# Modulation columns by one VectorE operation out of PSUM, two column blocks moved ahead of a matmul pass, one weight load moved ahead of another load

## The chip, the cores and the metric

The kernel runs on one core of a Trainium2 chip. The metric is the device time of one execution in microseconds (us). A core has a matmul engine (TensorE, in the profile PE, with its weight loads as PEld), a vector engine (VectorE, DVE), an activation engine (ScalarE, ACT), a general engine (GpSimd, POOL) and a queue engine that issues most transfers (SyncE, SP). Each engine works through its own instructions in order. SBUF is the on-chip memory, PSUM the memory that TensorE writes into.

## The reference

One transformer block on x of 1024 tokens by 1024 features, float32. What concerns this change is its beginning:

```python
mod = silu(c) @ w_ada + b_ada                      # 6 x 1024 numbers
sh_a, sc_a, g_a, sh_f, sc_f, g_f = split(mod, 6)
h = rms_norm(x, g_mix) * (1.0 + sc_a) + sh_a       # scale and shift by feature
proj = h @ w_in                                    # 1024 x 2240
# two kinds of attention on proj, w_out, residual times g_a,
# then rms_norm * (1 + sc_f) + sh_f, SwiGLU, residual times g_f, final rms_norm
```

So the first product needs, for every feature, two numbers that come from a product of c with w_ada: a scale g_mix * (1 + b + sc) and a shift b + sh. The features are cut into 8 blocks of 128, and the numbers of one block are two columns, one number for each of the 128 partitions.

## The kernel before

**The first pass.** A float32 product is made of three passes: each operand is split into a high part and the rest, and high*high, low*high and high*low are added in PSUM. In the code z = 0, 1, 2 are these three: pass (k, z) multiplies feature block k. `g1(0, ...)` (line 484 and on) does it for the first 512 tokens. For each k it runs the passes z = 0, 1, 2 over five output tiles at once (5 matmuls of 128x512 each, L481), and after each pass calls `between`, here `g1_0`, which puts the preparation of later blocks at that place of the program. Pass (k, 0) needs `hh` (high part of h, block k) and `whi` (high part of the weights), pass (k, 1) `hl`, pass (k, 2) `wlo`.

**What is made for one block k.** `h_T(0, k)` transposes x on TensorE into PSUM (L423). `ada_sum(c, ...)` (L255, L257) sums silu(c)[i] * w_ada[i] on VectorE, eight tiles one after the other, for a chunk c of columns: chunks 0 and 1 are one block wide, chunks 2, 4 and 6 are two blocks wide, so chunk 4 serves blocks 4 and 5. The partial sums lie in PSUM, the last one goes to SBUF as `acc`. `ada_cols(c)` adds the 128 partitions with small matmuls against ones (L270) and so makes the columns in PSUM. `acol_of` (L262 to L264) makes scale and shift from them and stores them in `acol`. `h_split(0, k)` applies both on ScalarE (L430, in place in PSUM), makes `hh` there (L162, a cast) and `hl` on VectorE (L158). The weights are split by `whi` (a cast on ScalarE, L303, that of tile 0 on GpSimd, L301) and `wlo` (a subtraction on GpSimd, L158).

**Order.** `pn` keeps what it is given in the order in which the code is written, so on each engine the work of this phase stands as `g1_0` calls it. `keep_busy` (L202) runs matmuls on constants into an unused tile. Transfers of this phase are issued by SP in the order of `load_x`, `load_ada` and `load_w` (from line 310). Tiles of 512 KB share one pool of 49 slots.

**After it** follow the rest of the projections, attention, the output product and the feed-forward part; the change touches none of them.

Of the kernel before, what the change touches and what calls it, by code (L numbers as in the profile page):

```python
# [11 lines left out]
ALU = mybir.AluOpType  # L12
# [85 lines left out]
def emit(ctx, tc, a, out, dbg=None, rec=None):  # L98
    nc = rec or tc.nc
# [11 lines left out]
    def slot(shape, dt, name):  # L111
        n = nm(name)
        if rec:
            rec.alloc(n)
        return sp.tile([P] + list(shape), dt, name=n, tag="s", bufs=NBUF)
# [37 lines left out]
    def pn(ins):  # L153
        if pinned[0]:
            pin(ins)
# [23 lines left out]
    V = con.tile([P, 78], F32, name="V")  # L179
    V1 = con.tile([P, 48], F32, name="V1")  # L180
    cact = con.tile([P, 8], F32, name="cact")
    acol = con.tile([P, 2, 8], F32, name="acol")
# [48 lines left out]
    def load_ada(k, q):  # L231
        n = CHUNKS[k]
        per = 4 // n
        src = a["ada_a"][k] if n == 1 else a["ada_b"][k // 2 - 1]
        adar[k, q] = slot([per, 256 * n], F32, "ada")
        pn(ld(out=adar[k, q], in_=src[:, q * per:(q + 1) * per, :]))
# [6 lines left out]
    def ada_sum(k, kts, sb=False):  # L243
        w = 256 * CHUNKS[k]
        if 0 in kts:
            adac[k] = [None, slot([512], F32, "acc"), None]
        e = adac[k]
        if not sb and e[0] is None:
            e[0] = psb()
        for kt in kts:  # L250
            src = ada_kt(k, kt)
            c = cact[:, kt:kt + 1]
            o = e[1] if sb or kt == 7 else e[0]
            if kt == 0:
                pn(nc.vector.tensor_scalar(out=o[:, 0:w], in0=src, scalar1=c, scalar2=None, op0=ALU.mult))  # L255
            else:
                pn(nc.vector.scalar_tensor_tensor(out=o[:, 0:w], in0=src, scalar=c, in1=e[2][:, 0:w], op0=ALU.mult, op1=ALU.add))  # L257
            e[2] = o

    def acol_of(k, n, sc, sh):  # L260
        ac = acol[:, 0, k:k + n]
        pn(nc.vector.tensor_tensor(out=ac, in0=sc, in1=V1[:, 8 + k:8 + k + n], op=ALU.add))  # L262
        pn(nc.vector.tensor_tensor(out=acol[:, 1, k:k + n], in0=sh, in1=V[:, 8 + k:8 + k + n], op=ALU.add))
        pn(nc.vector.tensor_tensor(out=ac, in0=ac, in1=V[:, 56 + k:56 + k + n], op=ALU.mult))  # L264

    def ada_cols(k):
        n = CHUNKS[k]
        ps, acc, _ = adac.pop(k)
        for s in range(2 * n):
            pn(mm(ps[:, s:s + 1], lhsT=acc[:, s * 128:(s + 1) * 128], rhs=ones[:, 0:1], start=True, stop=True))  # L270
        sc = ps[:, 0:2 * n].rearrange("p (k s) -> p s k", s=2)
        return lambda: acol_of(k, n, sc[:, 0, :], sc[:, 1, :])
# [21 lines left out]
    def load_w(k):  # L294
        raww[k] = slot([1024], F32, "raw")
        pn(ld(out=raww[k], in_=win[k * P:(k + 1) * P, 0:1024]))

    def whi(k, eng=None):
        W["s0", k] = (slot([1024], F32R, "whi"), slot([1024], F32R, "wlo"))
        if eng:  # L300
            pn(eng.tensor_copy(W["s0", k][0], raww[k]))  # L301
        else:
            pn(nc.scalar.copy(W["s0", k][0], raww[k]))  # L303

    def wlo(k):
        hi, lo = W["s0", k]
        sub(nc.gpsimd, lo, raww.pop(k), f(hi))
# [2 lines left out]
        load_x(t)  # L310
    load_ada(0, 0)
    load_ada(0, 1)
    load_ada(1, 0)
    load_w(0)
    load_ada(1, 1)
    load_w(1)
    for c in (2, 4, 6):
# [79 lines left out]
    for q in range(3):  # L397
        n = 3 if q < 2 else 2
# [21 lines left out]
    def h_T(hf, k, ts=range(4)):  # L420
        ps = hps[hf, k] = hps.get((hf, k)) or psb()
        for t in ts:
            pn(nc.tensor.transpose(ps[:, t * 128:(t + 1) * 128], xr[hf * 4 + t][:, k * 128:(k + 1) * 128], ident))  # L423

    def h_split(hf, k):
        ps = hps.pop((hf, k))
        if k % 2 == 0:
            hT[hf, k // 2] = (slot([2, 512], F32R, "hh"), slot([2, 512], F32R, "hl"))
        hi, lo = (z[:, k % 2, :] for z in hT[hf, k // 2])
        pn(nc.scalar.activation(ps, ps, AF.Identity, scale=acol[:, 0, k:k + 1], bias=acol[:, 1, k:k + 1]))  # L430
        split(ps, hi, lo)
# [107 lines left out]
    ada0((5, 6), True)  # L539
    keep_busy(4)  # L540
    acol_of(0, 1, ps0[:, 0, 0:1], ps0[:, 1, 0:1])
    ada_sum(1, range(2))
    whi(0, nc.gpsimd)
# [6 lines left out]
    def g1_0(k, z):  # L550
        if z == 0 and k < 7:
            h_T(0, k + 1)
        if z == 1 and k == 0:
            ada_sum(2, range(2))
            ada_cols(1)()
            ada_sum(2, range(2, 4))
            h_split(0, 1)
            ada_sum(2, range(4, 8))
            for j in (2, 3):
                whi(j)  # L560
                wlo(j)
        if z == 1 and k in (1, 3, 5):
            n = k + 3
            if n < 8:
                ada_sum(n, range(1))
            ada_cols(k + 1)()
            if n < 8:
                ada_sum(n, range(1, 3))
            h_split(0, k + 1)
            if n < 8:  # L570
                ada_sum(n, range(3, 6))
        if z == 1 and k in (2, 4, 6):
            h_split(0, k + 1)
            n = k + 2
            if n < 8:
                ada_sum(n, range(6, 8))
                for j in (n, n + 1):
                    whi(j)
                    wlo(j)
        if k == 6 and z == 1:  # L580
            st.ahead = 5
            st.allow(("ad", 2, 3))
            st.need(("x", 7))
# [5 lines left out]
    def g1_1(k, z):  # L589
# [4 lines left out]
        if z == 2:  # L594
            st.pump(2)

    g1(0, g1_0, g1_0t, 5)
    pinned[0] = False
    st.ahead = 4
# [87 lines left out]
    op = {}  # L687
# [80 lines left out]
    for u in range(2):  # L768
        nc.vector.tensor_tensor_reduce(out=lj, in0=lam[:, u * 128:u * 128 + 64], in1=lam[:, u * 128 + 64:u * 128 + 128],
                                       op0=ALU.mult, op1=ALU.add, scale=1.0, scalar=0.0, accum_out=lsum[:, u:u + 1])  # L770
# [782 lines left out]
```

## Time and profile before

| what | value |
|---|---|
| median of 3 executions | 1260.49 us (1259.66 to 1263.78) |
| profiled execution, its own time | 1262.53 us |
| its span, first to last instruction | 1260.5 us |
| mean granted TensorE clock | 0.982 |
| TensorE busy | 1209.6 us (96%) |
| VectorE, ScalarE, GpSimd busy | 830.9, 494.8, 439.0 us |
| first pass, blocks 0 to 7 | 16.23 to 62.5 us of the span |

The times of single instructions come from the profiled execution, whose own time is 2.0 us above its span and 2.0 us above the median. [...] In a timeline row the first number is the start, the second the time, and a bracket says how long the engine sat idle before it and what released it; rows of small float32 matmuls count each twice.

### The profile page before, as it was taken

To read this page: it belongs to the slowest core of one execution; us is meant where nothing else is said; L and a number is where in the kernel's file an instruction comes from. 1 tells how busy PE (TensorE), PEld (TensorE's weight loads), DVE (VectorE), ACT (ScalarE), POOL (GpSimd) and SP (SyncE) were. 2 spreads that over 40 slices of the span, in tenths; PEclk is the share of its full clock that TensorE was granted. 3 is DMA by queue.
4 is the path that set the end of the run, shared out by engine and by line. 5 is a ranking of instruction groups with operands and counts; after the bars stand their busy time and mean duration, and the time that the engine had idled before them with its cause. 6 is when DMAs were issued, how large, how long until landed. Compare 5 with 4: busy or idle time off the path is not lost.

```text
span 1260.5 us, 16480 instructions
## 1 busy us (share of the span) xinstructions
PE 1209.6 (96%) x5951; PEld 1016.3 (81%) x5951; DVE 830.9 (66%) x1284; ACT 494.8 (39%) x850; POOL 439.0 (35%) x492
## 2 busy tenths in 40 slices
PE   8999999999989999999899999999999999999995
PEld 6788898988779888887688888878888888878774
DVE  6552614567787778768865565655555665699997
ACT  4433314555546665214632233213233244243353
POOL 4312001655243247113465445564444620000112
PEclk9899999999999999999899999999999999999998
DMA  9672962347995434331132333322122369779543
GB/s 369 268 253 105 355 185 68 105 122 230 334 291 159 152 101 133 103 116 67 50 101 101 101 117 118 114 87 73 61 101 84 117 226 391 251 256 326 188 130 134
DMA packets 82972, 209.33 MB, mean 166 GB/s; under 512 B 7805, under 2 KB 18379, under 8 KB 82763
## 3 DMA queue, kind: packets, MB, share of 16 engines
q1 hardware_dynamic: 63611, 168.36, 40.0%
q0 software_dynamic: 6336, 23.07, 4.8%
q10 hardware_dynamic: 12944, 16.84, 3.9%
q8 instruction: 47, 0.77, 0.3%
q14 instruction: 34, 0.28, 0.1%
HBM read 164.21 MB, written 44.04 MB: 165 GB/s over the span
## 4 chain that ended last, share of the span: by engine, by line
PE 77%; DVE 12%; ACT 4%; issue 3%; DMA 2%; POOL 1%; SPq 0%; ACTq 0%; POOLq 0%; DVEq 0%
PE psb L1338 32%; PE psb L439 5%; PE psb L440 5%; PE psb L441 5%; PE psb L481 3%; PE psd L481 3%; PE psd L1485 2%; PE psd L1486 2%; PE psd L1484 2%; PE psb L1030 2%; PE psb L1485 2%; PE psb L1484 2%; PE psb L1486 2%; ACT s L949 2%; DVE dlo L158 1%
## 5 line engine op out<-in xcount | busy, mean ns | idle before, releaser
L1338 PE MATMUL psb<-ah,whi 128*128 128x512 f32 x528 | 143.6, 393 | 2.9 <-ACT uv L1367 2.6
L1338 PE MATMUL psb<-ah,wlo 128*128 128x512 f32 x528 | 141.9, 391 | 0.8 <-DVE wlo L158 0.8
L1338 PE MATMUL psb<-al,whi 128*128 128x512 f32 x528 | 141.7, 390 | 0.4 <-DVE al L158 0.4
L1361 POOL TENSOR_TENSOR cf<-cf,cf 128x512 f32<-128x512 f32 x44 | 66.4, 1510 | 190.4 <-DVE cf L1354 182.6
L1338 PEld LDWEIGHTS psb<-ah,whi 128*128 128x128 f32 x528 | 99.1, 189 | 25.0 <-ACT uv L1367 3.0
L1354 DVE TENSOR_TENSOR cf<-psb,uv 128x512 f32<-128x512 f32 x88 | 60.4, 687 | 89.0 <-PE psb L1338 87.6
L1338 PEld LDWEIGHTS psb<-ah,wlo 128*128 128x128 f32 x528 | 99.6, 189 | 22.1 <-DVE wlo L158 1.2
L1338 PEld LDWEIGHTS psb<-al,whi 128*128 128x128 f32 x528 | 99.0, 188 | 21.3 <-DVE al L158 0.8
L162 ACT CAST whi<-ssum 128x1024 fp32r<-128x1024 f32 x44 | 45.1, 1046 | 166.9 <-POOL ssum L158 166.9
L158 DVE TENSOR_TENSOR wlo<-ssum,whi 128x1024 fp32r<-128x1024 f32 x44 | 62.2, 1415 | 55.6 <-ACT whi L162 55.5
L949 ACT ACTIVATE s<-s,nb 128x640 f32<-128x640 f32 (+7 forms) x96 | 74.4, 776 | 48.2 <-DVE nb L947 47.7
L162 ACT CAST dhi<-raw 128x1024 fp32r<-128x1024 f32 x63 | 64.5, 1051 | 64.6 <-DVE raw L158 29.8
L947 DVE CUSTOM_DVE_ANT_0 s<-psd,tabs 128x640 f32<-128x640 f32 (+7 forms) x80 | 63.3, 804 | 36.5 <-PE psd L973 34.6
L158 DVE TENSOR_TENSOR dlo<-raw,dhi 128x1024 fp32r<-128x1024 f32 x59 | 73.9, 1276 | 15.5 <-ACT dhi L162 15.3
L1485 PE MATMUL psb<-dlo,dhi 128*128 128x512 f32 x176 | 69.0, 392 | 0.1
L1486 PE MATMUL psb<-dhi,dlo 128*128 128x512 f32 x176 | 68.5, 389 | 0.0
L439 PE MATMUL psb<-whi,hh 128*128 128x512 f32 (+2 forms) x192 | 67.4, 351 | 1.0 <-ACT latq L638 0.9
L1365 ACT ACTIVATE cf<-cf 128x512 f32<-128x512 f32 x44 | 27.8, 633 | 99.7 <-DVE cf L1354 99.7
L440 PE MATMUL psb<-wlo,hh 128*128 128x512 f32 (+2 forms) x192 | 66.6, 347 | 0.0
L441 PE MATMUL psb<-whi,hl 128*128 128x512 f32 (+2 forms) x192 | 66.6, 347 | 0.0
L1484 PE MATMUL psb<-dhi 128*128 128x512 f32 x176 | 63.8, 391 | 1.0 <-ACT dhi L162 0.8
L1453 POOL TENSOR_TENSOR x<-x,gfin 128x512 f32<-128x512 f32 x4 | 5.5, 1378 | 164.3 <-ACT o L1417 160.0
(322 smaller groups left out, 3117.4 us busy)
## 6 DMA issues: line engine op xcount, KB each, us to landing
adr<-in_w_ada_dram SPq DMA_DIRECT2D x32, 512.0 KB, 6.1
raw<-scr_g SPq DMA_DIRECT2D x55, 256.0 KB, 3.6
raw<-in_w_down_dram SPq DMA_DIRECT2D x55, 256.0 KB, 4.0
raw<-in_w_gate_dram SPq DMA_DIRECT2D x22, 512.0 KB, 3.3
raw<-in_w_up_dram SPq DMA_DIRECT2D x22, 512.0 KB, 3.4
scr_g<-cf POOLq DMA_DIRECT2D x22, 512.0 KB, 3.2
raw<-scr_g SPq DMA_DIRECT2D x22, 512.0 KB, 5.4
raw<-in_w_down_dram SPq DMA_DIRECT2D x22, 512.0 KB, 6.1
```

The source lines that it names most:

```text
L158: pn(eng.tensor_tensor(out=o, in0=x, in1=y, op=ALU.subtract))
L162: pn(nc.scalar.copy(hi, raw))
L439: mm(o, lhsT=ah, rhs=bh, start=start, stop=False)
L440: mm(o, lhsT=ah, rhs=bl, start=False, stop=False)
L441: mm(o, lhsT=al, rhs=bh, start=False, stop=stop)
L481: pn(mm(o, lhsT=w[z == 2][:, m * 128:(m + 1) * 128], rhs=h[z == 1], start=(k == 0 and z == 0), stop=(k == 7 and z == 2)))
L949: nc.scalar.activation(s, s, AF.Exp, bias=nb[:, m:m + 1], scale=-1.0, accum_out=rs[:, m:m + 1])
L1338: mm(o, lhsT=w[l][:, k, :], rhs=x[2 * (k // 2) + r][:, k % 2, :], start=(l + r == 0 and k == 0), stop=(r == 1 and k == 3))
L1361: nc.gpsimd.tensor_tensor(out=g, in0=g, in1=o, op=ALU.mult)
L1484: mm(o[t], lhsT=hi[:, 0, tt], rhs=hi[:, 1, :], start=c == 0, stop=False)
L1485: mm(o[t], lhsT=hi[:, 0, tt], rhs=lo[:, 1, :], start=False, stop=False)
L1486: mm(o[t], lhsT=lo[:, 0, tt], rhs=hi[:, 1, :], start=False, stop=c == NP - 1)
```

## The change

Three edits:

1. `acol_of` makes a scale column with one TENSOR_SCALAR that reads the sum from PSUM, adds one column and multiplies by another (both as scalars of each partition), one such operation for each block of the chunk. Before, one TENSOR_TENSOR added out of PSUM into `acol` (L262), and a second one multiplied in place in SBUF (L264). The shift's operation stays (L263 before, L264 after).
2. For blocks 3 and 5, `ada_cols` and what follows it in `g1_0` stand behind pass z = 0 instead of z = 1. For block 1 nothing moves.
3. `load_w(0)` is issued ahead of `load_ada(1, 0)` instead of behind it.

```diff
     def acol_of(k, n, sc, sh):
-        ac = acol[:, 0, k:k + n]
-        pn(nc.vector.tensor_tensor(out=ac, in0=sc, in1=V1[:, 8 + k:8 + k + n], op=ALU.add))
+        for j in range(k, k + n):
+            pn(nc.vector.tensor_scalar(out=acol[:, 0, j:j + 1], in0=sc[:, j - k:j - k + 1], scalar1=V1[:, 8 + j:9 + j],
+                                       scalar2=V[:, 56 + j:57 + j], op0=ALU.add, op1=ALU.mult))
         pn(nc.vector.tensor_tensor(out=acol[:, 1, k:k + n], in0=sh, in1=V[:, 8 + k:8 + k + n], op=ALU.add))
-        pn(nc.vector.tensor_tensor(out=ac, in0=ac, in1=V[:, 56 + k:56 + k + n], op=ALU.mult))
...
     load_ada(0, 1)
+    load_w(0)
     load_ada(1, 0)
-    load_w(0)
     load_ada(1, 1)
...
-        if z == 1 and k in (1, 3, 5):
+        if (k, z) in ((1, 1), (3, 0), (5, 0)):
```

TensorE in block 5, before: the transposes of block 6 (L423), pass (5, 1) with `hl` as its weights, the column matmuls of chunk 6 (L270), pass (5, 2).

```order
L423 MATMUL psb_470<-ident,x_115 128x128
L423 MATMUL psb_470<-ident,x_117 128x128
L481 MATMUL psd_270<-hl_420,whi_383 128x512 x2
L481 MATMUL psd_271<-hl_420,whi_383 128x512 x2
L481 MATMUL psb_272<-hl_420,whi_383 128x512
L270 MATMUL psb_408<-ones,acc_407 128x1 x4
L481 MATMUL psd_270<-hh_419,wlo_384 128x512 x2
```

The same place after:

```order
L423 MATMUL psb_468<-ident,x_115 128x128
L423 MATMUL psb_468<-ident,x_117 128x128
L270 MATMUL psb_401<-ones,acc_400 128x1 x4
L481 MATMUL psd_269<-hl_413,whi_381 128x512 x2
L481 MATMUL psd_270<-hl_413,whi_381 128x512 x2
L481 MATMUL psb_271<-hl_413,whi_381 128x512
L481 MATMUL psd_269<-hh_412,wlo_382 128x512 x2
```

The four column matmuls stand ahead of pass (5, 1), whose five matmuls are now queued behind them; block 3 has moved in the same way.

VectorE at the columns of chunk 4, before: the last sum of the chunk, the first product of chunk 6 (L255), the three operations of `acol_of`, the next sums.

```order
L257 SCALAR_TENSOR_TENSOR acc_334<-ada_149,cact,psb_335 128x512
L255 TENSOR_SCALAR psb_408<-ada_155,cact 128x512
L262 TENSOR_TENSOR acol<-psb_335,V_80 128x2
L263 TENSOR_TENSOR acol<-psb_335,V 128x2
L264 TENSOR_TENSOR acol<-acol,V 128x2
L257 SCALAR_TENSOR_TENSOR psb_408<-ada_155,cact,psb_408 128x512
```

The same place after:

```order
L257 SCALAR_TENSOR_TENSOR acc_332<-ada_149,cact,psb_333 128x512
L255 TENSOR_SCALAR psb_401<-ada_155,cact 128x512
L262 TENSOR_SCALAR acol<-psb_333,V_80,V 128x1 x2
L264 TENSOR_TENSOR acol<-psb_333,V 128x2
L257 SCALAR_TENSOR_TENSOR psb_401<-ada_155,cact,psb_401 128x512
```

The count stays at three for a chunk of two blocks (it falls from three to two for a chunk of one), the rest of VectorE's order stands as it was, and no operation of the three reads its tensor from SBUF any more.

SP's queue at the third edit, as a difference (`raw` is the weight tile, `ada` a tile of w_ada):

```order
 L236 DMA ada_121<-in_ada_a_dram 128x1024
-L236 DMA ada_123<-in_ada_a_dram 128x1024
-L296 DMA raw_125<-in_w_in_dram 128x1024
+L296 DMA raw_123<-in_w_in_dram 128x1024
+L236 DMA ada_125<-in_ada_a_dram 128x1024
 L236 DMA ada_127<-in_ada_a_dram 128x1024
```

Weight tile 0 and the first tile of chunk 1 change places; everything behind them keeps its place.

## Rows read from the trace of the kernel before

**Rows 1.** The page: busy times by engine, and granted clock in 40 slices

```profile
PE 1209.6 (96%) x5951; PEld 1016.3 (81%) x5951; DVE 830.9 (66%) x1284; ACT 494.8 (39%) x850; POOL 439.0 (35%) x492
...
PEclk9899999999999999999899999999999999999998
```

**Rows 2.** Waits of TensorE, 0 to 62 us: total, times, longest

```profile
PE psd L481 <- ACT hh L162: 4.7, 4, 1.7
```

**Rows 3.** Stretches from one pass (k, 0) to the next, blocks 1, 2, 4, 5, 6

```profile
core 0: us, PE busy (x) PEld busy (x) DVE busy (x) ACT busy (x) POOL busy (x), PEclk, DMA share, GB/s
...
23.10:30.89 7.79, 5.36 (x28) 3.95 (x28) 7.13 (x12) 3.44 (x4) 4.71 (x2) 0.94 1.03 407
30.89:37.58 6.69, 6.69 (x19) 5.35 (x20) 4.71 (x7) 3.23 (x4) 0.91 (x1) 0.56 1.02 408
...
43.17:47.16 3.99, 3.99 (x20) 3.31 (x20) 3.52 (x6) 2.05 (x3) 0.00 (x0) 1.00 1.03 410
47.16:53.74 6.58, 4.93 (x29) 3.92 (x27) 2.77 (x6) 2.53 (x4) 4.73 (x2) 1.00 0.38 150
53.74:59.34 5.60, 5.60 (x20) 4.57 (x20) 1.38 (x2) 2.19 (x3) 0.00 (x0) 0.70 0.26 56
```

**Rows 4.** Timeline of TensorE in blocks 1 to 6

```profile
26.85 1.05 PE L270 MATMUL psb<-ones,acc 128*128 128x1 f32 x8 [0.73 <-DVE acc L257]
...
30.89 2.07 PE L481 MATMUL psd<-hh,whi 128*128 128x512 f32 x4 [1.70 <-ACT hh L162]
...
43.17 1.19 PE L481 MATMUL psd<-hh,whi 128*128 128x512 f32 x4 [0.65 <-ACT hh L162]
...
48.65 1.17 PE L481 MATMUL psd<-hl,whi 128*128 128x512 f32 x4
...
49.89 0.95 PE L270 MATMUL psb<-ones,acc 128*128 128x1 f32 x8
50.70 1.16 PE L481 MATMUL psd<-hh,wlo 128*128 128x512 f32 x4
...
53.74 2.06 PE L481 MATMUL psd<-hh,whi 128*128 128x512 f32 x4 [1.65 <-ACT hh L162]
```

**Rows 5.** Timeline of VectorE at the columns of chunks 2, 4 and 6

```profile
26.71 0.75 DVE L255 TENSOR_SCALAR psb<-ada,cact 128x512 f32<-128x512 f32 x1
27.94 0.16 DVE L262 TENSOR_TENSOR acol<-psb,V 128x2 f32<-128x2 f32 x1 [0.48 <-PE psb L270]
...
28.14 1.23 DVE L264 TENSOR_TENSOR acol<-acol,V 128x2 f32<-128x2 f32 x1
...
41.49 0.16 DVE L264 TENSOR_TENSOR acol<-acol,V 128x2 f32<-128x2 f32 x1
...
47.87 0.75 DVE L257 SCALAR_TENSOR_TENSOR acc<-ada,cact,psb 128x512 f32<-128x512 f32 x1
50.88 0.16 DVE L262 TENSOR_TENSOR acol<-psb,V 128x2 f32<-128x2 f32 x1 [2.26 <-PE psb L270]
...
51.07 1.15 DVE L264 TENSOR_TENSOR acol<-acol,V 128x2 f32<-128x2 f32 x1
```

**Rows 6.** Timeline of GpSimd in blocks 1, 3 and 5

```profile
24.64 4.71 POOL L158 TENSOR_TENSOR wlo<-raw,whi 128x1024 fp32r<-128x1024 f32 x2 [4.03 <-ACT whi L303]
36.67 4.74 POOL L158 TENSOR_TENSOR wlo<-raw,whi 128x1024 fp32r<-128x1024 f32 x2 [7.31 <-ACT whi L303]
47.48 4.73 POOL L158 TENSOR_TENSOR wlo<-raw,whi 128x1024 fp32r<-128x1024 f32 x2 [6.07 <-ACT whi L303]
```

**Rows 7.** Timeline of ScalarE ahead of pass (6, 0)

```profile
52.31 0.75 ACT L430 ACTIVATE psb<-psb,acol 128x512 f32<-128x512 f32 x1 [3.96 <-DVE acol L264]
```

**Rows 8.** Timeline of all engines around pass (0, 0)

```profile
14.57 1.04 POOL L301 CAST whi<-raw 128x1024 fp32r<-128x1024 f32 x1 [2.98 <-DMA raw<-in_w_in_dram]
14.58 0.48 DVE L255 TENSOR_SCALAR psb<-ada,cact 128x256 f32<-128x256 f32 x1
...
15.55 0.59 ACT L162 CAST hh<-psb 128x512 fp32r<-128x512 f32 x1
...
16.17 0.69 DVE L158 TENSOR_TENSOR hl<-psb,hh 128x512 fp32r<-128x512 f32 x1 [0.58 <-ACT hh L162]
...
16.23 2.04 PE L481 MATMUL psd<-hh,whi 128*128 128x512 f32 x4 [0.80 <-POOL whi L301]
```

**Rows 9.** Waits of TensorE, 62 to 200 us

```profile
PE psb L669 <- ACT latq L638: 1.6, 1, 1.6
```

## Prediction

> **What bounds the kernel now.** First the page: TensorE is busy for 1209.6 of 1260.5 us, so a change can gain only where TensorE idles or runs at a lower clock, and the granted clock is below full speed in three places, one of them the second slice [rows 1]. Next the waits of TensorE in the first 62 us, where all three edits lie: most of the idle time is four waits of pass (k, 0) for `hh`, 4.7 us together, the longest 1.7 [rows 2]. The timeline shows three of the four: 1.70 ahead of block 2, 0.65 ahead of block 4, 1.65 ahead of block 6 [rows 4]. They are the even blocks, whose columns come from a new chunk. Last the stretches from block to block: block 4 takes 3.99 us with TensorE always busy at full clock, blocks 2 and 6, with the same work, take 6.69 and 5.60 at a mean clock of 0.56 and 0.70 [rows 3]. [...] After 62 us TensorE waits once in 138 us, for 1.6 [rows 9]: what the first pass gains is carried on.
>
> **Why `hh` is late.** The chain ahead of pass (6, 0) is: column matmuls at 49.89, `acol_of` from 50.88 to 52.22 (51.07 + 1.15), L430 at 52.31, the cast, pass (6, 0) at 53.74 [rows 4, 5, 7]. Two things in it are too long. The column matmuls stand behind pass (5, 1), though their input `acc` was ready at 48.62 (47.87 + 0.75), just as that pass began (48.65) [rows 4, 5]. And L264, 256 numbers, took 1.15 us, in chunk 2 even 1.23, against 0.16 in chunk 4 [rows 5]. GpSimd says why: its two `wlo` subtractions end at 29.35, 41.41 and 52.21 [rows 6]. The slow L264 end at 29.37 and 52.22, within 0.02 of GpSimd's end; the quick one began at 41.49, after it. L262, which reads one input from PSUM, took 0.16 both times while GpSimd ran. So the operation with both inputs in SBUF was held until GpSimd was done.
>
> **Edit 1, the columns.** It removes L264 five times. What comes is a TENSOR_SCALAR that reads its tensor from PSUM and two scalars from SBUF. The trace has no such form. Nearest rows: L262, 0.16, from PSUM (lower bound); L264, 1.23, if the two scalars count as SBUF inputs (upper bound). L255 is a TENSOR_SCALAR with a scalar from SBUF; it ran at 26.71, in the middle of GpSimd's work, and took 0.75 for 512 columns, without being held [rows 5, 6]. I take 0.16, the row that shares the PSUM input. Three operations started 0.1 apart (27.94 to 28.14), so in chunk 2 the last one would end at 28.14 + 0.16 = 28.30 instead of 29.37: 1.07 earlier. In chunks 0 and 1 one operation of that spacing falls out, 0.1 each; there VectorE is on the path, since block 1 has it busy for 7.13 of 7.79 us [rows 3], so I count 0.2.
>
> [...] The rows say that here the count is not what costs: the same L264 took 0.16 and 1.23.
>
> **What follows in block 2.** Pass (2, 0) starts 1.07 earlier and its wait shrinks from 1.70 to 0.63. That is the length of the wait ahead of block 4 (0.65), behind which the clock stayed at 1.00 [rows 3, 4]. I therefore expect block 2 at full clock: 3.99 instead of 6.69, a gain of 2.70. This is the least sure term: block 1 has another wait of 0.73 ahead of its column matmuls [rows 4], which block 3 does not have, and it stays.
>
> **Edit 2, the moved columns.** In blocks 3 and 5 the chain starts one pass earlier. For block 5 by its own rows: column matmuls from 48.65, they take 0.81 of TensorE (49.89 to 50.70); the columns are there 0.99 after their start (49.89 to 50.88), so `acol_of` runs from 49.64 to 50.0; from L430 to the pass it is 1.43 (52.31 to 53.74), so `hh` is ready at about 51.5 [rows 4, 5, 7]. TensorE is done with passes (5, 1) and (5, 2) at 52.09 as before (53.74 - 1.65). So `hh` is 0.6 early and the wait of 1.65 goes; with the same arithmetic the 0.65 ahead of block 4 goes. With no wait the clock stays up in block 6: 3.99 instead of 5.60, a gain of 1.61 [rows 3].
>
> What it costs: the column matmuls now wait for `acc` with pass (k, 1) queued behind them. `acc` came 0.03 before TensorE would get there, so there is no room. VectorE has 0.36 us of `acol_of` to do earlier than before, and its sums were ready in time with TensorE at full clock in blocks 4 and 5, which is the pace I expect for blocks 2 and 3 as well. I put 0.1 for each of the two places. GpSimd's `wlo` overlaps the moved `acol_of`; by the value taken in edit 1 that costs nothing, and without it up to 2.4 at each place (one of the two subtractions, 4.73 / 2).
>
> **Edit 3, the load.** Weight tile 0 comes one tile earlier. `whi` ran on GpSimd from 14.57 to 15.61, but `hh` was ready only at 15.55 + 0.59 = 16.14, and the pass began at 16.23: the bracket names GpSimd, yet `hh` came last [rows 8]. So nothing is gained. The w_ada tile takes the place of the weight tile and is there at about 14.57; L255, which reads it, began at 14.58. A small delay there is hidden, since VectorE then idles 0.58 ahead of `hl` [rows 8]. I count 0.
>
> **Sum.** 0.2 (chunks 0, 1) + 1.07 (block 2) + 2.70 (its clock) + 0.65 (block 4) + 1.65 (block 6) + 1.61 (its clock) - 0.2 (waits for `acc`) = 7.7 us. Against the profiled execution's own time: 1262.53 - 7.7 = **1254.8 us**. That execution was 2.0 above the median of 1260.49; that the shown runs spread from 1259.66 to 1263.78 fits executions that lose the clock once, twice or not at all. Against the median the gain is 5.7 us, 0.45%. Less than 0.3% (3.8 us) can't be told from no change here.
>
> **Rivals.**
> 1. The clock falls in block 2 all the same. [...] Then 2.70 is lost from the sum: 1262.53 - 5.0 = 1257.5. [...]
> 2. The edit does not do what it says: TENSOR_SCALAR with scalars from SBUF is held by GpSimd as L264 was. Then block 2 keeps its wait and its clock; the columns of block 5 end when GpSimd does, at 52.2 as now; in block 3 the end moves from 41.65 to 41.41. The gain is 0.2 + 0.24, and the time 1262.1. Against it stands L255 in rows 5.
> 3. The gain is given back later, since loads further on, not TensorE, set the pace. Half given back is 1258.7, all 1262.5. Against it: rows 9.
> 4. Slower: the moved column matmuls hold up TensorE. If `acc` comes 1.7 late in blocks 3 and 5 (the longest wait in rows 2), and the clock falls behind each as in block 2 (2.70) and in block 2 itself, then -5.0 + 2 x (1.7 + 2.7) = +3.8, or 1266.3. It turns against the change from 2.5 us lost at each place, and is slower than the median by 0.3% (1264.3) from 3.4. Against it: `acc` at 48.62 for a pass at 48.65.
>
> **How the numbers follow.** Forecast 0.60, rival 1 0.24, rival 2 0.06, rival 3 0.06, rival 4 0.04. The range goes from 2 us below the forecast (0.2 of unused allowance, a scatter like that of the runs shown) to beyond rivals 1 and half of 3: 1252.8 to 1259.2. Faster by over 0.3% is below 1256.7: the forecast and a quarter of rival 1, 0.66. Within 0.3%: the rest of rival 1, rivals 2 and 3, 0.29. Slower: rival 4 and a bit of scatter, 0.05.
>
> **What the profile after would show.** Edit 1: no operation of `acol_of` over 0.3 us, in chunk 2 while GpSimd runs. Block 2: a wait of about 0.6 and four matmuls in 1.2 us, not 2.1. Edit 2: no wait for `hh` ahead of blocks 4 and 6, waits for `acc` of at most 0.3 at the moved matmuls, and block 6 in about 4.0. Edit 3: `whi` on GpSimd about 1.3 earlier (one tile of 512 KB at the 410 GB/s that block 4 shows [rows 3]) and pass (0, 0) within 0.1 of 16.2. The end of the first pass at about 54.8 instead of 62.5. I am wrong if `acol_of` is still held, if TensorE waits for `acc` by more than 0.5, or if the first pass is 7 us shorter and the span is not.

## The result and the profile after

The changed kernel takes 1255.62 us (median of 8 executions, 1251.64 to 1257.75); the kernel before, timed beside it, 1261.14 (8 executions, 1259.12 to 1265.11). The ratio is 0.9946, 95% interval 0.9930 to 0.9961: 0.5% faster. 1254.8 us was predicted.

The profiled execution after took 1257.22 us, with a span of 1255.3. Its stretches from block to block, for the same blocks 1, 2, 4, 5 and 6 as in [rows 3] (columns as there):

```profile
22.93:29.82 6.89, 5.35 (x27) 3.95 (x27) 6.22 (x12) 3.44 (x4) 4.71 (x2) 1.00 1.02 407
29.82:33.87 4.05, 4.04 (x19) 3.32 (x20) 3.57 (x6) 2.09 (x3) 0.00 (x0) 1.00 1.04 414
38.65:42.54 3.89, 3.89 (x21) 3.21 (x20) 3.39 (x6) 2.08 (x3) 0.22 (x1) 1.00 1.01 405
42.54:47.33 4.79, 4.79 (x29) 4.10 (x28) 2.04 (x6) 2.48 (x4) 4.51 (x2) 1.00 1.03 411
47.33:51.23 3.90, 3.90 (x20) 3.20 (x20) 1.26 (x2) 2.08 (x3) 0.22 (x1) 1.00 0.85 296
```

From the start of pass (2, 0) to the end of block 7 (29.82 to 54.63) TensorE is busy for 24.80 of 24.81 us, at full clock (mean granted clock 1.00). The waits of TensorE in the first 62 us:

```profile
PE psd L481 <- ACT hh L162: 2.1, 2, 1.3
...
PE psb L270 <- DVE acc L257: 0.7, 1, 0.7
```

Against 4.7 us in four waits [rows 2] two waits for `hh` are left, ahead of blocks 1 and 2. The timeline of TensorE:

```profile
22.93 1.20 PE L481 MATMUL psd<-hh,whi 128*128 128x512 f32 x4 [1.30 <-ACT hh L162]
...
29.82 1.21 PE L481 MATMUL psd<-hh,whi 128*128 128x512 f32 x4 [0.81 <-ACT hh L162]
...
38.65 1.07 PE L481 MATMUL psd<-hh,whi 128*128 128x512 f32 x4
...
44.11 0.96 PE L270 MATMUL psb<-ones,acc 128*128 128x1 f32 x8
...
47.33 1.09 PE L481 MATMUL psd<-hh,whi 128*128 128x512 f32 x4
```

Passes (4, 0) and (6, 0) have no wait in front. The wait ahead of block 1 is 1.30 because block 0 got its full clock back sooner than before (mean clock 0.81 from 16.08 to 21.63, before 0.72 from 16.23 to 22.42) and so ended earlier; block 1 still starts at 22.93 (before: 23.10). VectorE at the columns of chunks 2 and 6, and GpSimd:

```profile
27.78 0.46 DVE L262 TENSOR_SCALAR acol<-psb,V,V 128x1 f32<-128x1 f32 x2 [0.48 <-PE psb L270]
28.16 0.15 DVE L264 TENSOR_TENSOR acol<-psb,V 128x2 f32<-128x2 f32 x1
...
43.22 0.75 DVE L257 SCALAR_TENSOR_TENSOR acc<-ada,cact,psb 128x512 f32<-128x512 f32 x1
45.11 0.47 DVE L262 TENSOR_SCALAR acol<-psb,V,V 128x1 f32<-128x1 f32 x2 [1.15 <-PE psb L270]
45.49 0.15 DVE L264 TENSOR_TENSOR acol<-psb,V 128x2 f32<-128x2 f32 x1
```

```profile
24.75 4.71 POOL L158 TENSOR_TENSOR wlo<-raw,whi 128x1024 fp32r<-128x1024 f32 x2 [4.02 <-ACT whi L303]
34.14 4.73 POOL L158 TENSOR_TENSOR wlo<-raw,whi 128x1024 fp32r<-128x1024 f32 x2 [4.68 <-ACT whi L303]
42.82 4.73 POOL L158 TENSOR_TENSOR wlo<-raw,whi 128x1024 fp32r<-128x1024 f32 x2 [3.95 <-ACT whi L303]
```

Both chunks' columns now fall in GpSimd's work (24.75 to 29.46, 42.82 to 47.55) and nothing is held: where L264 took 1.23 and 1.15 [rows 5], the two TENSOR_SCALAR take 0.46 together and the shift 0.15. `acc` of chunk 6 is ready at 43.97, its matmuls begin at 44.11, right behind the transposes.

The first pass, from the start of pass (0, 0) to the end of block 7, takes 38.55 us (16.08 to 54.63) instead of 46.51 (16.23 to 62.74): 7.96 less. The two profiled executions differ by 5.31 (1262.53 to 1257.22). Matched instruction by instruction along TensorE, the rest is given back in two stretches far behind the first pass. Before and after:

```profile
195.91:260.70 64.79, 61.33 (x407) 58.95 (x406) 33.23 (x100) 34.35 (x106) 30.59 (x89) 0.97 0.37 100
345.33:353.67 8.34, 4.82 (x27) 4.41 (x26) 5.54 (x10) 2.39 (x7) 2.59 (x5) 0.82 1.02 397
```

```profile
187.81:254.06 66.25, 62.82 (x407) 60.43 (x406) 32.85 (x98) 34.28 (x106) 30.51 (x89) 0.95 0.34 97
339.05:348.59 9.54, 4.96 (x28) 4.55 (x27) 5.69 (x10) 2.53 (x7) 2.73 (x5) 0.68 1.03 390
```

The stretches take 1.46 and 1.20 longer, but not for the same cause. In the first, TensorE is busy 1.49 us longer with the same matmuls, at a lower mean clock. In the second its busy time grows by only 0.14; the rest is idle time. TensorE waits there for VectorE (L988), and VectorE, where the `ptl` of that wait stands behind a sum (L341), stands still until the tile of w_ada for this sum has come from memory: 3.50 us after, 2.44 before. First before, then after:

```profile
348.61 1.28 DVE L341 SCALAR_TENSOR_TENSOR acc<-adr,cact,acc 128x1024 f32<-128x1024 f32 x1 [2.44 <-DMA adr<-in_w_ada_dram]
350.55 0.54 PE L988 MATMUL psb<-E,E 128*128 128x384 f32 x1 [2.94 <-DVE ptl L158]
```

```profile
343.39 1.28 DVE L341 SCALAR_TENSOR_TENSOR acc<-adr,cact,acc 128x1024 f32<-128x1024 f32 x1 [3.50 <-DMA adr<-in_w_ada_dram]
345.33 0.69 PE L988 MATMUL psb<-E,E 128*128 128x384 f32 x1 [4.00 <-DVE ptl L158]
```

Whether the change brings this about was the first question for the experiments.

### The profile page after: what moved, and what is told of

It is laid out like the page before. It is cut to its first block, busy times and chain, and to the rows that moved or that the text cites. A ratio compares the mean times of both kernels' runs of the same rounds, so it can differ in the third digit from the quotient of the medians.

```text
span 1255.3 us, 16479 instructions
## 1 busy us (share of the span) xinstructions
PE 1205.8 (96%) x5951; PEld 1013.7 (81%) x5951; DVE 829.2 (66%) x1282; ACT 494.4 (39%) x850; POOL 439.0 (35%) x492
## 4 chain that ended last, share of the span: by engine, by line
PE 77%; DVE 12%; ACT 4%; issue 4%; DMA 1%; POOL 1%; SPq 0%; ACTq 0%; POOLq 0%; DVEq 0%
PE psb L1338 32%; PE psb L439 5%; PE psb L441 5%; PE psb L440 5%; PE psb L481 3%; PE psd L481 3%; PE psd L1485 2%; PE psd L1486 2%; PE psd L1484 2%; PE psb L1030 2%; ACT s L949 2%; PE psb L1485 2%; PE psb L1484 2%; PE psb L1486 2%; DVE dlo L158 1%
```

## The experiments

The theory: an operation of VectorE with both tensors in SBUF is held while GpSimd works; that delays `hh`, and the idle time of TensorE costs a second time when the clock falls behind it (in the kernel before the granted clock is 1.00 in block 4, 0.50 from 31.0 to 36.5 in block 2 and from 54.0 to 57.0 in block 6). The rivals: the moved matmuls did it; the smaller number of operations did it; the clock falls for another reason. All are judged by the first pass, which the trace gives to 0.1 us, and by the ratio to the kernel before (all executions of one kernel), which tells some 0.2% (2.5 us) apart. The first pass and its clock are those of one profiled execution of each kernel.

| kernel | first pass us | its mean clock | ratio to before (95%) |
|---|---|---|---|
| before | 46.51 | 0.85 | 1 |
| before, again | 45.53 | 0.93 | one execution, 1261.30 us |
| changed | 38.55 | 0.97 | 0.9946 (0.9930 to 0.9961) |
| changed, again | 38.85 | 0.96 | one execution, 1255.06 us |
| edit 1 alone | 42.64 | 0.91 | 0.9933 (0.9907 to 0.9959) |
| edit 2 alone | 44.29 | 0.94 | 0.9982 (0.9965 to 1.0000) |
| edit 3 alone | 46.71 | 0.85 | 0.9998 (0.9979 to 1.0017) |
| edits 1 and 2 | 40.01 | 0.91 | 0.9943 (0.9924 to 0.9963) |
| sum back into PSUM | 40.50 | 1.00 | 0.9959 (0.9939 to 0.9978) |
| product with one SBUF tensor | 40.42 | 1.00 | one execution, 1254.11 us |
| before, waits filled | 43.69 | 0.93 | 0.9986 (0.9971 to 1.0002) |
| changed, half of chunk 1 on TensorE | 41.30 | 0.92 | 0.9950 (0.9932 to 0.9968) |
| changed, waits filled | 38.56 | 1.00 | 0.9944 (0.9926 to 0.9962) |

**Edit 1 alone** (`acol_of` as in the change, all else as before).

> Edit 1 alone: the scale columns by one operation out of PSUM; the column matmuls of blocks 3 and 5 and the load stay where they were. Theory (the operation with two SBUF inputs was held by GpSimd, and its delay cost idle time and the clock): no operation of acol_of over 0.3 us; pass (2, 0) starts at about 29.8 instead of 30.9 and runs at clock 1.00; the waits for hh ahead of blocks 4 and 6 are both about 0.8 (0.65 plus 0.17, since the two new operations take 0.23 each), with block 6 at clock 1.00; the first pass ends at about 56.4 instead of 62.5, and 4 to 6 us of time go. Rival (the moved columns are what counted): waits of 1.6 ahead of block 6 and the low clock behind it stay, and less than 2 us go.

Measured: no operation of `acol_of` is held; waits of 0.82, 0.82 and 0.83 ahead of blocks 2, 4 and 6, block 6 at full clock, as expected. Block 2 was not at full clock: it ran at a mean clock of 0.70 behind a wait of 0.82, where the changed kernel had full clock behind 0.81.

```profile
32.02:37.62 5.60, 5.60 (x20) 4.54 (x20) 3.95 (x6) 2.48 (x4) 0.11 (x1) 0.70 1.03 410
```

So the first pass came out 2.3 longer than the expected 40.3 (16.1 to 56.4), of which this block is 1.55 (5.60 against 4.05), and the time still fell by 0.67%, the largest fall of those with an interval. By time, edit 1 alone can't be told from the whole change.

**Edit 2 alone** (`if (k, z) in ((1, 1), (3, 0), (5, 0))`, `acol_of` as before).

> Edit 2 alone: column matmuls of blocks 3 and 5 behind pass z = 0; acol_of in three operations with the product in place in SBUF, as before. Theory: the moved product now falls into GpSimd's work in block 3 as well and ends within 0.05 us of the end of one of its two subtractions, in block 5 too; block 2 keeps its wait of 1.7 and its low clock; the first pass ends between 61.7 and 62.5, and 0 to 1 us goes. Rival (moving alone takes the waits away): no wait ahead of blocks 4 and 6 and block 6 at clock 1.00, first pass at 58.6, 3.9 us less.

Measured: the products of chunks 2, 4 and 6, and GpSimd's work:

```profile
28.21 1.34 DVE L264 TENSOR_TENSOR acol<-acol,V 128x2 f32<-128x2 f32 x1
...
39.44 1.61 DVE L264 TENSOR_TENSOR acol<-acol,V 128x2 f32<-128x2 f32 x1
...
49.36 2.28 DVE L264 TENSOR_TENSOR acol<-acol,V 128x2 f32<-128x2 f32 x1
```

```profile
24.82 4.72 POOL L158 TENSOR_TENSOR wlo<-raw,whi 128x1024 fp32r<-128x1024 f32 x2 [4.00 <-ACT whi L303]
36.30 4.73 POOL L158 TENSOR_TENSOR wlo<-raw,whi 128x1024 fp32r<-128x1024 f32 x2 [6.77 <-ACT whi L303]
46.88 4.75 POOL L158 TENSOR_TENSOR wlo<-raw,whi 128x1024 fp32r<-128x1024 f32 x2 [5.85 <-ACT whi L303]
```

They end at 29.55, 41.05 and 51.64, GpSimd at 29.54, 41.03 and 51.63. In chunk 4, where the product had taken 0.16 behind GpSimd's work [rows 5], moving it forward put it into that work, and it is held as well. The waits ahead of blocks 4 and 6 stay, at 0.96 and 1.59 (before: 0.65 and 1.65). Where the expectation fell short is the clock: block 6 ran at full clock behind nearly the same wait (4.03 instead of 5.60), and block 2 was at the lower clock for a shorter time (5.60 instead of 6.69), which makes the pass shorter (60.59 at its end) than expected. The rival falls: without edit 1 the move takes no wait away.

**The sum back into PSUM** (three operations as before, one SBUF input less).

```diff
-        pn(nc.vector.tensor_tensor(out=ac, in0=sc, in1=V1[:, 8 + k:8 + k + n], op=ALU.add))
+        pn(nc.vector.tensor_tensor(out=sc, in0=sc, in1=V1[:, 8 + k:8 + k + n], op=ALU.add))
...
-        pn(nc.vector.tensor_tensor(out=ac, in0=ac, in1=V[:, 56 + k:56 + k + n], op=ALU.mult))
+        pn(nc.vector.tensor_tensor(out=ac, in0=sc, in1=V[:, 56 + k:56 + k + n], op=ALU.mult))
```

> The kernel before with the same three operations in acol_of, but the first one writes its sum back into PSUM and the product reads it from there (one SBUF input instead of two). Theory (two SBUF inputs are what GpSimd holds up): the product takes 0.16 in all five places, and the first pass ends at about 56.2, as with edit 1 alone or a little sooner. Rival (what helped was one operation in place of two): the product still takes 1.15 to 1.23 in chunks 2 and 6 and the first pass ends at 62.5.

Measured: the product takes 0.15 each time, in chunks 2 and 6 with GpSimd at work from 25.09 to 29.82 and from 44.22 to 48.96.

```profile
28.57 0.15 DVE L264 TENSOR_TENSOR acol<-psb,V 128x2 f32<-128x2 f32 x1
...
47.93 0.15 DVE L264 TENSOR_TENSOR acol<-psb,V 128x2 f32<-128x2 f32 x1
```

With the number of operations unchanged the hold is gone. What counts here is whether both tensors lie in SBUF: 1.23 and 1.15 in the kernel before, 0.15 with one of them in PSUM.

**The product with one SBUF tensor** (TENSOR_SCALAR in place in SBUF, the factor as a scalar of each partition).

```diff
-        pn(nc.vector.tensor_tensor(out=ac, in0=ac, in1=V[:, 56 + k:56 + k + n], op=ALU.mult))
+        for j in range(k, k + n):
+            pn(nc.vector.tensor_scalar(out=acol[:, 0, j:j + 1], in0=acol[:, 0, j:j + 1], scalar1=V[:, 56 + j:57 + j], scalar2=None,
+                                       op0=ALU.mult))
```

> The kernel before, with the product of acol_of as a TENSOR_SCALAR in place in SBUF: one tensor input in SBUF, the factor as a scalar of each partition, one such operation for each block. Theory (what GpSimd holds up is a second tensor read from SBUF): none of the eight takes over 0.3 us, also while GpSimd runs, and the first pass is shorter by 3.5 to 6 us than before (46.3 from the start of pass (0, 0)). Rival (any operation that reads its tensor from SBUF is held): 0.6 to 2.4 us each in chunks 2 and 6, first pass as before.

Measured: none of the eight takes over 0.22; the pairs of chunks 2 and 6 take 0.34 and 0.33 together, both times inside GpSimd's work (25.00 to 29.73 and 44.14 to 48.88); the first pass is 40.42.

```profile
28.45 0.34 DVE L265 TENSOR_SCALAR acol<-acol,V 128x1 f32<-128x1 f32 x2
...
47.77 0.33 DVE L265 TENSOR_SCALAR acol<-acol,V 128x1 f32<-128x1 f32 x2
```

So these small operations with a tensor and a scalar from SBUF are not held; the product of two tensors is (1.23 and 1.15 in the kernel before). Larger operations of this kind were not tried beside this GpSimd work.

**The waits filled** (the kernel before, six matmuls into an unread PSUM tile behind passes (1, 2) and (5, 2)).

```diff
+                if hf == 0 and k in (1, 5) and z == 2:
+                    junk = psb()
+                    for _ in range(6):
+                        pn(mm(junk, lhsT=W["s0", k][0][:, 0:128], rhs=h_op(0, k)[0], start=True, stop=True))
```

> The kernel before with six more matmuls of 128x512 behind pass (1, 2) and behind pass (5, 2), into a PSUM tile that nobody reads: about 1.4 us of work in waits of 1.70 and 1.65. No chain is shortened. Theory (the low clock comes from the idle time ahead of blocks 2 and 6 and is a cost of its own): pass (2, 0) still starts at 30.9 and the products of acol_of still take 1.15 to 1.23, but blocks 2 and 6 run at clock 1.00 in about 4.0 us each; the first pass ends at about 58.2 instead of 62.5 and 2 to 4.3 us go (other executions may lose the clock less often than the profiled one). Rival (the clock falls for another reason): blocks 2 and 6 stay at 6.7 and 5.6 and the time is the same.

Measured: blocks 2 and 6 at full clock, though the products are held as before (0.67 and 1.15):

```profile
35.45:39.39 3.94, 3.94 (x20) 3.24 (x20) 3.48 (x6) 2.09 (x3) 0.00 (x0) 1.00 1.02 408
56.52:60.55 4.03, 4.03 (x19) 3.32 (x20) 1.39 (x2) 2.08 (x3) 0.00 (x0) 1.00 0.32 77
```

In this execution, then, the low clock went with the idle time. One execution alone doesn't show that filling is what did it, since the clock also stays up behind some long waits: here behind one of 1.63 ahead of block 4, which was not filled. Counted over the thirteen profiled executions (blocks 1 to 7; one wait of 0.25 left out), the clock was low in the block behind seven of the nine waits of 1.59 to 1.87 us and behind four of the 29 waits of 0.64 to 1.37. In the 52 blocks that began without a wait, pass (k, 0) always ran at full clock (four matmuls in 1.07 to 1.12 us). That bears the theory out as a matter of odds, not as a rule for a single wait.

The end expected at 58.2 came at 63.95. Of these 5.75 us, 4.03 are a late beginning: transfers came later (GpSimd's cast, which waits for weight tile 0, began at 15.19 instead of 14.57), the product of chunk 0 was held (1.86 us), and pass (0, 0) started at 20.26. The rest lies mainly in block 0, which ran at the lower clock for longer (7.88 us instead of 6.87), and in block 4: the product of chunk 4 now fell into GpSimd's work (39.67 to 44.41) and was held too, and the wait ahead of block 4 grew from 0.65 to 1.63.

```profile
43.30 1.12 DVE L264 TENSOR_TENSOR acol<-acol,V 128x2 f32<-128x2 f32 x1
```

```profile
45.94 1.20 PE L481 MATMUL psd<-hh,whi 128*128 128x512 f32 x4 [1.63 <-ACT hh L162]
```

The time shows no gain that can be told from none (0.9986, up to 1.0002), so the price of the clock in the time is not shown by this run.

**Edit 3 alone, and the change without it.**

> Edit 3 alone: weight tile 0 loaded ahead of chunk 1, acol_of with its product in SBUF as before. Theory (two SBUF inputs are held by GpSimd): GpSimd's work on tile 0 now runs from about 13.4 to 16.9 us, so the product of chunk 0, which began at 14.51 just ahead of that work, is held until about 14.5 or 16.9; pass (0, 0) starts up to 2.4 us later, at about 18.6, the first pass ends at about 64.9, and the kernel is 0 to 2.5 us slower. Rival (as the prediction had it for the whole change: the load is free): the product takes 0.16, pass (0, 0) starts at 16.2, no difference.

Missed: the product of chunk 0 took 0.15. It began at 14.74, in the gap of 0.09 between GpSimd's cast (13.65 to 14.69) and its subtraction (from 14.78). Pass (0, 0) at 16.45 and no difference in time.

> Edits 1 and 2 without edit 3. Theory (no operation of acol_of is held any more, and hh comes later than whi): the same first pass as with all three edits, 38.5 us from the start of pass (0, 0), which starts at about 16.1; ratio to before 0.993 to 0.997. Rival (the earlier load is worth something): pass (0, 0) starts 0.5 us or more later than with edit 3.

Measured: pass (0, 0) at 16.03, ratio 0.9943, the same as with edit 3. The first pass took 40.01 instead of the expected 38.5: block 2 fell to the lower clock here behind a wait of 0.83:

```profile
29.79 2.07 PE L481 MATMUL psd<-hh,whi 128*128 128x512 f32 x4 [0.83 <-ACT hh L162]
```

That is the whole difference from the changed kernel (38.55): block 2 takes 5.51 instead of 4.05.

**Half of chunk 1 on TensorE** (4 of its 8 tiles as matmuls of 128x1 in `ada1_cols`, called behind pass (0, 0)).

> All three edits, and half of chunk 1's sums (4 of 8 tiles) as small matmuls on TensorE in place of VectorE, its columns behind pass (0, 0). Theory (blocks 0 to 2 are now bound by VectorE's sums, which 1.3 us of wait ahead of block 1 and 0.7 for acc in block 1 show): VectorE has 2.1 us less to do ahead of chunk 2, the wait ahead of block 1 goes, pass (2, 0) starts 0.8 to 1.6 us earlier than 29.8; the whole is 1 us faster than with the three edits, too little for the timing to tell. Rival (those blocks wait for the transfers of w_ada): pass (2, 0) at 29.8 as before.

Missed: pass (2, 0) started at 30.06. VectorE had less to do and then stood still: the first product of chunk 4, which stands ahead of chunk 2's columns, waited for its tile.

```profile
27.36 0.75 DVE L255 TENSOR_SCALAR psb<-ada,cact 128x512 f32<-128x512 f32 x1 [0.97 <-DMA ada<-in_ada_b_dram]
```

In this execution the transfers are next in line behind VectorE in blocks 0 to 2: it stood still for 0.89 and 0.97 us for tiles of w_ada. The wait ahead of block 1 did go, but behind 1.28 us ahead of block 2 the clock fell, and that block took 6.63, most of what the first pass is longer (41.30). The time is that of the change.

**Both kernels again, unchanged.**

> The changed kernel once more, unchanged, to see which parts of its time differ from execution to execution. Theory (what is given back behind the first pass is a matter of where the clock falls, not a consequence of the change): the first pass takes 38.5 us from the start of pass (0, 0), or up to 2.8 more where the clock falls in block 2; the stretch from about 188 to 254 us, which took 66.2, and that from 339 to 349, which took 9.5, come out elsewhere between 63.4 and 66.3 and between 4.5 and 9.6. Rival (a consequence of the change): 66.2 and 9.5 again.

> The kernel before once more, unchanged. Theory: the first pass takes 42 to 46.7 us by where the clock falls (both falls 46.5, none 42.2); the product of chunks 2 and 6 is held until GpSimd's subtraction ends; the stretch that took 64.8 us comes out between 63.4 and 66.3. Rival (the falls of the clock belong to the waits alone): 46.5 again, with low clock in blocks 2 and 6.

Measured: first pass 38.85 and 45.53. In the kernel before the hold is there again (1.39 and 1.13), and blocks 2 and 6 are again at the lower clock for part of their time. In block 2 it fell one pass later than in the first profile: pass (2, 0) ran at full clock behind a wait of 1.87 (four matmuls in 1.20 us), pass (2, 1) at the lower (2.06). That is why this first pass is 1 us shorter than 46.51. It fits the theory, and nearly the rival too.

```profile
31.11:36.73 5.62, 5.62 (x20) 4.59 (x20) 4.60 (x7) 3.15 (x4) 0.79 (x1) 0.70 1.03 409
52.90:58.43 5.53, 5.53 (x19) 4.54 (x20) 1.38 (x2) 2.10 (x3) 0.00 (x0) 0.70 0.26 57
```

In the changed kernel the clock fell in block 1 this time, behind a wait of 1.32; in its first profile it had stayed up there behind 1.30.

```profile
23.18 2.08 PE L481 MATMUL psd<-hh,whi 128*128 128x512 f32 x4 [1.32 <-ACT hh L162]
```

The two far stretches, first the changed kernel, then the kernel before:

```profile
188.35:253.30 64.95, 61.50 (x407) 59.12 (x405) 32.89 (x98) 34.28 (x106) 30.50 (x89) 0.97 0.37 100
338.33:346.43 8.10, 4.85 (x28) 4.43 (x27) 5.57 (x10) 2.42 (x7) 2.61 (x5) 0.82 1.02 394
```

```profile
195.01:259.75 64.74, 61.28 (x407) 58.92 (x406) 33.23 (x100) 34.31 (x106) 30.50 (x89) 0.97 0.36 100
344.74:352.62 7.88, 4.81 (x28) 4.39 (x27) 5.53 (x10) 2.38 (x7) 2.57 (x5) 0.82 1.02 400
```

This time they differ by 0.2 each, the first passes by 6.68, and the times by 6.24 (1261.30 to 1255.06): the first pass accounts for it. The wait for the w_ada tile in the second stretch (L341) is 2.17 and 1.99 here. Of the thirteen profiled executions, the five with edits 1 and 2 have it at 1.71 to 3.50 and the others at 1.99 to 2.96, but for edit 1 alone, where the tile was there in time and the stretch took 4.50. So this wait differs from execution to execution, and nothing shows that the change lengthens it.

**The changed kernel, waits filled** (`keep_busy(6)` in place of 4 ahead of pass (0, 0), two unread matmuls behind pass (0, 2), three behind pass (1, 2)).

> The changed kernel with matmuls that nobody reads in its remaining waits: two more ahead of pass (0, 0), two ahead of pass (1, 0), three (0.7 us) ahead of pass (2, 0), where the wait is 0.8. Theory (the clock in block 2 falls in some executions behind that wait, at 1.5 to 2.8 us each): block 2 runs at clock 1.00 in about 4.0 us, the first pass takes 38.4 to 38.7 us, and the time is 0 to 1.5 us below that of the changed kernel, ratio to before 0.993 to 0.996. Rival (the fill delays the passes behind it, or the clock does not depend on it): first pass over 39 us.

Measured: there is no wait ahead of block 2, which takes 4.02 us at full clock (30.33 to 34.35); first pass 38.56, ratio 0.9944. The lowest first pass is reached, not undercut, and the time can't be told from that of the change.

## Why the prediction was right, step by step

- **What bounds, and why `hh` is late**: right. The hold by GpSimd rests on more than coincidence now: it follows the product when it is moved into GpSimd's work (edit 2 alone) and goes when one of the two tensors leaves SBUF, with the count unchanged. In numbers: 0.67 to 2.28 us where it began inside a GpSimd subtraction, 0.15 to 0.16 where it did not. That the number of operations is not what costs was read from one trace; the sum back into PSUM shows it: same count, first pass 40.50 instead of 46.51.
- **Edit 1**: the kind right, the size off by a little. The two TENSOR_SCALAR take 0.46 and `acol_of` 0.53 (27.78 to 28.31) instead of the 0.36 that went into the sum; pass (2, 0) started 1.07 earlier (30.89 to 29.82) instead of 1.27, of which 0.15 is the earlier start of pass (0, 0), and its wait was 0.81, not 0.63. The upper bound, 1.23 for scalars that count as SBUF inputs, is not what happens.
- **The clock in block 2**, 2.70: right in the profiled execution (4.05 instead of 6.69), but not a fixed term. Behind waits of 0.82 and 0.83 it fell in two other executions of kernels with edit 1, at 1.5 us each, and in the kernel before, repeated, it fell one pass later (block 2 took 5.62). So rival 1 is no rival but what happens in some executions, and that this one had full clock is in part luck.
- **Edit 2**: the effect right, its share wrong. Both waits gone, no wait for `acc`; the 0.2 kept for it was not needed. Block 6 takes 3.90. The prediction's "up to 2.4 at each place" without edit 1 is what edit 2 alone showed (1.61 and 2.28). What it had wrong is the split: it gave edit 2 the whole 1.65 ahead of block 6 and the 1.61 of its clock, 3.7 in all with block 4 and less the 0.2. But edit 1 takes the hold out of chunk 6 as well: without edit 2 the waits ahead of blocks 4 and 6 were 0.70 to 0.83, and block 6 was at full clock three times out of three (edit 1 alone, sum back into PSUM, product with one SBUF tensor). Removing the hold brings the first pass from 46.51 to 40.50 (sum back into PSUM), the whole change to 38.55 at nearly the same clock (1.00 and 0.97): 2.0 is left for edit 2, too little to be told by the times.
- **Edit 3**: right, nothing.
- **The sum**: 7.7 against 7.96 measured in the first pass. Small misses cancel in it: edit 1 gave 0.35 less than its 1.27 (0.92 without the earlier start), while the 0.2 kept for `acc` was not needed and blocks 3 to 6 each gave 0.1 to 0.2 more than counted.
- **What the first pass gains is carried on**: this held to 188 us and was the weakest reading. It rested on the waits up to 200 us [rows 9], while two later stretches differ from execution to execution: the first between 63.4 and 66.2 over the thirteen profiled executions, with a mean clock of 1.00 to 0.95, the second between 4.50 and 9.54 in five of them. In the profiled execution they took 2.66 back; in the repeated pair almost nothing. That the change lengthens the first is not shown, and not excluded: 66.2 was seen twice, both times with edits 1 and 2, but the other three executions with these edits had 64.95, 65.01 and 63.44. Rival 3 was right about part of what it named: of the 2.66, 1.06 is a longer wait for a load; the rest is mostly the clock. The prediction's sum put both at nothing, and by its own last sign (first pass 7 us shorter, the span not) it came out between: 7.96 and 5.2.
- **The time**: 1254.8 lies within 1 us of the median, 1255.62, but 2.4 below the profiled execution (1257.22). The sum was taken off one profiled execution that lay above the median and had the low clock in both blocks, and it left out what the later stretches can take back. That these offset each other in the median is partly luck. From median to median 5.5 us were gained; the prediction's 5.7 against the median is near for the same reason.

## What to carry to other kernels

Look for a tiny VectorE operation that takes a microsecond: if both its tensors lie in SBUF and its end coincides with the end of a GpSimd instruction, read one of the two from PSUM, or make it a scalar of each partition (here 0.15, or 0.33 to 0.34 for two operations, in place of 1.15 and 1.23). A wait of TensorE is to be priced with the clock behind it, and that second price differed between executions (block 2 of the kernel before took 6.69 us and, repeated, 5.62, against 3.99 for block 4), so the span of one profile is not the measure of a change; the stretch that the change touches is. An operation moved forward may land in a neighbour's work, as the product of chunk 4 did in edit 2 alone (1.61 instead of 0.16): check what runs there before counting the wait as gone.

## What the runs showed of the hardware

- A small VectorE product of two SBUF tensors (256 numbers, once 128) took 0.67 to 2.28 us where it began inside a GpSimd subtraction (2.36 us each), thirteen times ending within 0.02 us of the end of that subtraction. Beside the same GpSimd work the product took 0.15 with one tensor from PSUM, and 0.33 to 0.34 as two operations with one tensor and a scalar from SBUF.
- In all thirteen cases no GpSimd instruction followed right behind that subtraction. A place where one did stands far behind the first pass in the kernel before. A VectorE subtraction of two SBUF tensors took 1.21 with no GpSimd operation beside it, and 2.30 where it began inside one; it ended 1.08 after that one (653.36 to 654.44), and GpSimd's next, begun at 653.32, took 2.28 instead of the 1.29 of one with no VectorE operation beside it. In this one place, then, both were longer.

```profile
592.63 1.21 DVE L158 TENSOR_TENSOR wlo<-ssum,whi 128x1024 fp32r<-128x1024 f32 x1
...
652.14 2.30 DVE L158 TENSOR_TENSOR wlo<-raw,whi 128x1024 fp32r<-128x1024 f32 x1
```

```profile
651.73 1.63 POOL L158 TENSOR_TENSOR ssum<-ssum,raw 128x512 f32<-128x512 f32 x1
653.32 2.28 POOL L158 TENSOR_TENSOR ssum<-raw,raw 128x512 f32<-128x512 f32 x1
...
682.91 1.29 POOL L158 TENSOR_TENSOR ssum<-raw,raw 128x512 f32<-128x512 f32 x1
```

- Behind waits of nearly the same length TensorE came back at the lower clock in one execution and at full clock in another of the same kernel (the changed kernel, pass (1, 0): 2.08 us for four matmuls behind 1.32, 1.20 behind 1.30). Where the granted clock was read over such four matmuls, 2.07 us went with 0.50 (the kernel before, 30.89 to 32.96) and 1.20 us with 1.00 (the changed kernel, 22.93 to 24.13).
